# Seven block products instead of eight in the up projection of an MLP, with the residual kept in DRAM

## The chip, the core and the metric

The kernel runs on one core of a Trainium2 chip. What counts is the device time of one execution, in microseconds (us). The engines of the core work side by side, each through its own list of instructions in order: TensorE (PE; its weight loads are listed as PEld), VectorE (DVE), ScalarE (ACT), GpSimd (POOL) and SyncE (SP). TensorE reads SBUF and writes PSUM, which has eight banks of 512 float32 columns; VectorE and ScalarE read both. Transfers between DRAM and SBUF are started from the queues of SP, ACT and POOL.

## The reference

One layer of a decoder with 512 tokens and 2048 features, all in float32. A gated linear attention mixer comes first, then the MLP, then a gated embedding and a last norm. The MLP, which the change is about, is:

```python
def sq_relu_mlp(u, w_up, w_down):
    return jnp.square(jax.nn.relu(u @ w_up)) @ w_down
...
        h = h + mix.astype(h.dtype)
        h = h + sq_relu_mlp(rmsnorm(h, norm_mlp[i]), w_up[i], w_down[i])
```

`w_up` is 2048 x 8192 and `w_down` 8192 x 2048. `rmsnorm` divides each token by the root mean square of its features and multiplies by a gain.

## The kernel before

**Three products for one.** To reach float32 accuracy, each operand is split exactly into two parts of a shorter type, float32r: `hi`, a cast on ScalarE, and `lo`, the rest, a subtraction on VectorE. `mm3` (L134 to L138) then adds up hi·hi, hi·lo and lo·hi. Each of these matmuls names its stationary tile (128 x 128 of the weights in the MLP) and streams the other operand.

**Weights.** `load_w` (L122) loads a block of 512 KB, four k tiles of 128 rows x 256 columns, on SP's queue (three buffers, `raw`), casts it on ScalarE (`whi`, four buffers) and subtracts on VectorE (`wlo`, four buffers).

**Projections.** `proj_a` (L147) makes 256 output features at a time for all 512 tokens: two PSUM banks of 128 features x 512 tokens, over all k tiles, 24 matmuls for each block of weights; then `evac` reads the banks. The banks come from two pools: `mm` with six and `at` with two.

**The MLP.** After the output projection, `evac_out` (L677) adds the residual x, which lies in DRAM (`xT_d`), and keeps the sum `h` in eight SBUF tiles. `gain_split` multiplies it by the gain and splits it into `U`; the token's root mean square is put in later, as the row `r2`. The hidden features are taken in eight slices of 1024 (FFC, L31). For each slice the up projection (L705) runs over 16 k tiles; `evac_up` multiplies by `r2` with the relu, squares and splits into `S`. Then the down projection (L712) runs over the slice's eight k tiles, and `evac_dn` adds to `h` in place. The last slice also makes the gain and split for the next stage, the gate projection, whose last two column groups are 256 wide (GROUPS, L737).

**Order.** The program order is that of the loops, but the framework that builds the kernel lays out each engine's list itself: it takes an instruction when its inputs and its buffer are due, earlier instructions of the program first. It also sets all semaphores, and gives out buffers of a pool as they come free. The largest pool is `spool` with 34 slots of 4 KB per partition.

## Time and profile before

| what | before |
|---|---|
| median of 3 runs | 2435.47 us (2435.34 to 2437.28) |
| the profiled execution: its span, first to last instruction | 2433.7 us (the only time that is given for it) |
| TensorE busy | 2416.9 us, 99% |
| VectorE busy | 1049.6 us, 43% |
| ScalarE busy | 720.3 us, 30% |
| moved by DMA | 248 MB, 102 GB/s |

The profile comes from one more execution, so its span is set beside the median and not taken for it. Busy time is counted for each engine by itself; the engines overlap. An engine's idle time is put down to what ended it. Names are those of the program, with buffer numbers left out: `ps_up` stands for all PSUM tiles of the up projection. A line number is that of the innermost helper, so L136 to L138 are the three matmuls of `mm3` wherever they are called.

### The profile page before, as it was taken

To read this page: it belongs to the slowest core of one execution; us is meant where nothing else is said; L and a number is where in the kernel's file an instruction comes from. 1 tells how busy PE (TensorE), PEld (TensorE's weight loads), DVE (VectorE), ACT (ScalarE), POOL (GpSimd) and SP (SyncE) were. 2 spreads that over 40 slices of the span, in tenths; PEclk is the share of its full clock that TensorE was granted. 3 is DMA by queue.
4 is the path that set the end of the run, shared out by engine and by line. 5 is a ranking of instruction groups with operands and counts; after the bars stand their busy time and mean duration, and the time that the engine had idled before them with its cause. 6 is when DMAs were issued, how large, how long until landed. Compare 5 with 4: busy or idle time off the path is not lost.

```text
span 2433.7 us, 26605 instructions
## 1 busy us (share of the span) xinstructions
PE 2416.9 (99%) x11056; PEld 2010.0 (83%) x11056; DVE 1049.6 (43%) x1402; ACT 720.3 (30%) x923; POOL 42.9 (2%) x79
## 2 busy tenths in 40 slices
PE   9999999999999999999999999999999999999998
PEld 7888888888888888888888888888888888888888
DVE  6655647446644433333333333333333333354344
ACT  5433324333433321221222221221221222233322
POOL 3000000000100000000000000000000000000000
PEclk9999999999999999999999999999999999999999
DMA  7323323223344333333333323333333333333222
GB/s 256 100 78 109 87 78 104 87 91 91 119 128 126 119 101 97 95 95 96 98 101 96 96 95 97 102 96 95 95 96 99 100 96 95 104 97 115 91 78 79
DMA packets 219017, 248.18 MB, mean 102 GB/s; under 512 B 8308, under 2 KB 197424, under 8 KB 218896
## 3 DMA queue, kind: packets, MB, share of 16 engines
q1 hardware_dynamic: 213344, 228.68, 30.8%
q0 software_dynamic: 5520, 17.79, 2.2%
q8 instruction: 86, 1.41, 0.2%
q14 instruction: 35, 0.29, 0.0%
q10 hardware_dynamic: 32, 0.01, 0.0%
HBM read 234.91 MB, written 11.53 MB: 101 GB/s over the span
## 4 chain that ended last, share of the span: by engine, by line
PE 87%; issue 11%; DMA 0%; DVE 0%; POOL 0%; ACT 0%; SPq 0%; ACTq 0%; POOLq 0%
PE ps_up L136 10%; PE ps_up L138 10%; PE ps_dn L138 10%; PE ps_dn L137 10%; PE ps_dn L136 10%; PE ps_up L137 10%; PE ps_g L136 2%; PE ps_g L138 2%; PE ps_g L137 2%; PE ps_wo L137 2%; PE ps_wo L138 2%; PE ps_wo L136 2%; PE ps_v L136 1%; PE ps_v L137 1%; PE ps_og L137 1%
## 5 line engine op out<-in xcount | busy, mean ns | idle before, releaser
L136 PE MATMUL ps_up<-U_norm_mlp,whi_up 128*128 128x512 f32 x1024 | 398.9, 390 | 0.0
L138 PE MATMUL ps_up<-U_norm_mlp,wlo_up 128*128 128x512 f32 x1024 | 398.4, 389 | 0.0
L137 PE MATMUL ps_up<-U_norm_mlp,whi_up 128*128 128x512 f32 x1024 | 398.3, 389 | 0.0
L136 PE MATMUL ps_dn<-S,whi_dn 128*128 128x512 f32 x1024 | 398.3, 389 | 0.0
L137 PE MATMUL ps_dn<-S,whi_dn 128*128 128x512 f32 x1024 | 398.3, 389 | 0.0
L138 PE MATMUL ps_dn<-S,wlo_dn 128*128 128x512 f32 x1024 | 398.3, 389 | 0.0
L128 DVE TENSOR_TENSOR wlo_up<-raw_up,whi_up 128x1024 fp32r<-128x1024 f32 x128 | 156.8, 1225 | 347.3 <-ACT whi_up L126 347.3
L126 ACT CAST whi_up<-raw_up 128x1024 fp32r<-128x1024 f32 x128 | 135.0, 1055 | 519.6 <-PE ps_up L137 380.2
L126 ACT CAST whi_dn<-raw_dn 128x1024 fp32r<-128x1024 f32 x128 | 135.0, 1054 | 516.7 <-PE ps_dn L137 384.6
L128 DVE TENSOR_TENSOR wlo_dn<-raw_dn,whi_dn 128x1024 fp32r<-128x1024 f32 x128 | 156.8, 1225 | 275.2 <-ACT whi_dn L126 275.2
L137 PEld LDWEIGHTS ps_up<-U_norm_mlp,whi_up 128*128 128x128 f32 x1024 | 192.2, 188 | 40.1 <-issue 0.2
L138 PEld LDWEIGHTS ps_up<-U_norm_mlp,wlo_up 128*128 128x128 f32 x1024 | 192.2, 188 | 40.0
L136 PEld LDWEIGHTS ps_up<-U_norm_mlp,whi_up 128*128 128x128 f32 x1024 | 192.2, 188 | 40.0 <-issue 0.2
L137 PEld LDWEIGHTS ps_dn<-S,whi_dn 128*128 128x128 f32 x1024 | 192.2, 188 | 39.9
L138 PEld LDWEIGHTS ps_dn<-S,wlo_dn 128*128 128x128 f32 x1024 | 192.2, 188 | 39.9
L136 PEld LDWEIGHTS ps_dn<-S,whi_dn 128*128 128x128 f32 x1024 | 192.2, 188 | 39.9
L708 DVE TENSOR_TENSOR h<-h,ps_dn 128x512 f32<-128x512 f32 x128 | 87.5, 687 | 170.9 <-PE ps_dn L138 170.9
L136 PE MATMUL ps_g<-whi_wg,U_norm_ple 128*128 128x512 f32 (+1 forms) x320 | 112.0, 350 | 0.0
L138 PE MATMUL ps_g<-whi_wg,U_norm_ple 128*128 128x512 f32 (+1 forms) x320 | 111.3, 348 | 0.0
L137 PE MATMUL ps_g<-wlo_wg,U_norm_ple 128*128 128x512 f32 (+1 forms) x320 | 111.2, 348 | 0.0
L136 PE MATMUL ps_og<-X,whi_og 128*128 128x512 f32 x256 | 102.5, 400 | 0.0
L136 PE MATMUL ps_v<-whi_v,X 128*128 128x512 f32 x256 | 100.8, 394 | 0.0
(270 smaller groups left out, 3307.9 us busy)
## 6 DMA issues: line engine op xcount, KB each, us to landing
raw_up<-in_w_up SPq DMA_DIRECT2D x128, 512.0 KB, 3.7
raw_dn<-in_w_down SPq DMA_DIRECT2D x128, 512.0 KB, 3.6
raw_v<-in_gla_w_in SPq DMA_DIRECT2D x32, 512.0 KB, 3.8
raw_og<-in_gla_w_in SPq DMA_DIRECT2D x32, 512.0 KB, 3.8
raw_wo<-in_gla_w_out SPq DMA_DIRECT2D x32, 512.0 KB, 3.5
raw_wg<-in_w_ple_gate SPq DMA_DIRECT2D x32, 512.0 KB, 3.7
raw_q<-in_gla_w_in SPq DMA_DIRECT2D x12, 512.0 KB, 3.7
raw_k<-in_gla_w_in SPq DMA_DIRECT2D x12, 512.0 KB, 3.8
```

What stands on the lines that cost most here:

```text
L126: nc.scalar.copy(hi, raw)
L128: nc.vector.tensor_tensor(out=lo, in0=raw, in1=hi.bitcast(F32), op=ALU.subtract)
L136: nc.tensor.matmul(ps, lhsT=wa[0], rhs=wb[0], start=first, stop=False)
L137: nc.tensor.matmul(ps, lhsT=wa[0], rhs=wb[1], start=False, stop=False)
L138: nc.tensor.matmul(ps, lhsT=wa[1], rhs=wb[0], start=False, stop=last)
L708: nc.vector.tensor_tensor(out=h_of(i), in0=h_of(i), in1=ps, op=ALU.add)
```

## The change

The up projection is computed by Strassen's scheme on 2 x 2 blocks: two k tiles by two feature tiles of the weights, and two k tiles by two halves of 256 tokens of the input. Seven block products take the place of eight. They need sums and differences of blocks on both sides.

- **The input's side**, once: `operands` makes four differences of the scaled residual for each pair of k tiles, and splits these and three of the blocks themselves. The root mean square of the attention's input (`rb`) is put in here, and its inverse (`rinv`) later, in `r2`. This stands in the output projection's `evac_out`, for the last three pairs behind it.
- **The weights' side**, for each of 32 groups of 256 features: `up_group` loads blocks of 512 KB as before. VectorE makes four sums for each pair of k tiles (three operations for two pairs, in one buffer, `sum`). ScalarE casts three blocks and four sums for each pair, VectorE subtracts. 21 matmuls of 256 columns follow for each pair. The seven products lie in halves of four PSUM banks.
- **The evacuation**: a copy on ScalarE and five operations on VectorE put the four output blocks together, then relu with `r2`, square and split as before, on 1024 columns at once.
- **The slices** become 16 chunks of 512 hidden features. A chunk's two up groups alternate with the eight down groups of the chunk before: block, block, down, block, down, block, down, evacuation, down, and the same again. The first chunk has no down groups, the last round only these.
- **The residual** no longer lies in SBUF. `evac_out` stores it to a new DRAM tensor `h_d`; each down group loads its two tiles (256 x 512) on POOL's queue, adds its two banks, and stores them back. The last chunk keeps them in SBUF. Even down groups take banks from `mm`, odd ones from `at`.
- **Room**: some buffers of the attention are closed before the MLP, the buffers for temporaries are fewer, and the memory for POOL's descriptors is a quarter of what it was. One early load of many small pieces, `lr_raw`, moves from POOL's queue to ScalarE's.

```diff
-FFC = 1024
+FFC = 512
+NKP = NK // 2
+HT = T // 2
...
+    h_d = dram.tile([NK, P, T], F32, name="h_d")
...
             lr_raw = slot([P, NK, RANK], "lr_raw")
-            nc.gpsimd.dma_start(lr_raw, w_in[:, 6144:6160].rearrange("(k p) c -> p k c", p=P))
+            nc.scalar.dma_start(lr_raw, w_in[:, 6144:6160].rearrange("(k p) c -> p k c", p=P))
...
+            nc.vector.tensor_scalar(out=rinv, in0=ssum, scalar1=1.0 / D, scalar2=EPS, op0=ALU.mult, op1=ALU.add)
+            nc.vector.tensor_tensor(out=rinv, in0=rinv, in1=rtok, op=ALU.mult)
             bcast(rtok, rb, "x")
...
     scope.close()
-    tpool = ctx.enter_context(tc.tile_pool(name="tpool", bufs=6))
+    mlp = ExitStack()
+    tpool = mlp.enter_context(tc.tile_pool(name="tpool", bufs=1))
+    def extra(shape, name, dtype=F32):
+        return spool2.tile(shape, dtype, tag="e", name=name)
+    def wide(name):
+        return tpool.tile([P, 8, HT], F32, tag="w", name=name)
+    def sums(name):
+        return tpool.tile([P, 2, 4, P], F32, tag="sum", name=name)
...
+    def operand_slots(kp):
+        a_ = [slot([P, 4, HT], f"XS{p}_{kp}", F32R) for p in range(2)]
+        if kp % 2 == 0:
+            b_ = [slot([P, 4, HT], f"XA{p}_{kp}", F32R) for p in range(2)]
+            spare[kp + 1] = b_
+            runs = [[(0, 3, b_[p][:, 0:3, :])] for p in range(2)]
+        else:
+            e = slot([P, 4, HT], f"XA_{kp}", F32R)
...
+    def operands(kp, u):
+        a_, runs = operand_slots(kp)
+        ub = u.rearrange("p k (h t) -> p (k h) t", h=2)
+        d = sums(f"D_{kp}").rearrange("p a b c -> p (a b c)").rearrange("p (o t) -> p o t", t=HT)
+        nc.vector.tensor_tensor(out=d[:, 0, :], in0=ub[:, 1, :], in1=ub[:, 3, :], op=ALU.subtract)
+        nc.vector.tensor_tensor(out=d[:, 1, :], in0=ub[:, 0, :], in1=ub[:, 1, :], op=ALU.subtract)
+        nc.vector.tensor_tensor(out=d[:, 2, :], in0=ub[:, 0, :], in1=d[:, 0, :], op=ALU.subtract)
+        nc.vector.tensor_tensor(out=d[:, 3, :], in0=ub[:, 2, :], in1=d[:, 2, :], op=ALU.subtract)
+        for n_run in range(len(runs[0])):
+            o, n, hi = runs[0][n_run]
+            lo = runs[1][n_run][2]
+            for q_ in range(n):
+                blk = (0, 2, 3)[o + q_]
+                if q_ and (0, 2, 3)[o + q_ - 1] == blk - 1:
+                    continue
+                m = 2 if q_ + 1 < n and (0, 2, 3)[o + q_ + 1] == blk + 1 else 1
+                src = ub[:, blk:blk + m, :]
+                nc.scalar.copy(hi[:, q_:q_ + m, :], src)
+                nc.vector.tensor_tensor(
+                    out=lo[:, q_:q_ + m, :], in0=src, in1=hi[:, q_:q_ + m, :].bitcast(F32), op=ALU.subtract)
+        nc.scalar.copy(a_[0], d)
+        nc.vector.tensor_tensor(out=a_[1], in0=d, in1=a_[0].bitcast(F32), op=ALU.subtract)
+    late = {}
+    def evac_out(i, ps):
+        kp = i // 2
+        if i % 2 == 0:
+            late["x"] = load([P, 2, T], f"xres_{kp}")
+            nc.gpsimd.dma_start(late["x"], xT_d[i:i + 2].rearrange("k p t -> p k t"))
+            if kp in (5, 6):
+                late["u"] = extra([P, 2, T], f"u_{kp}")
+            else:
+                late["u"] = wide(f"u_{kp}").rearrange("p a t -> p (a t)").rearrange("p (a t) -> p a t", t=T)[:, 0:2, :]
+            late[kp] = late["u"]
+        h = late["x"][:, i % 2, :]
+        nc.vector.tensor_tensor(out=h, in0=ps, in1=h, op=ALU.add)
+        nc.vector.scalar_tensor_tensor(
+            out=late["u"][:, i % 2, :], in0=h, scalar=vec("norm_mlp", i), in1=rb, op0=ALU.mult, op1=ALU.mult)
+        add_squares(h, f"mlp_{i}", i == 0)
+        if i % 2:
+            nc.gpsimd.dma_start(h_d[i - 1:i + 1].rearrange("k p t -> p k t"), late["x"])
+            if kp < 5:
+                operands(kp, late["u"])
+    w_out = a["gla_w_out"].rearrange("o k c -> (o k) c")
+    proj_a(w_out, 0, GH, 0, D, evac_out, None, "wo")
+    for kp in (5, 6, 7):
+        operands(kp, late[kp])
+    r2 = const.tile([P, T], F32, name="r2")
+    rt2 = tiny([P, NTT], "rt2")
+    nc.vector.tensor_tensor(out=rt2, in0=rstd_of(token_sums(acc2, "mlp"), D, NTT, "mlp"), in1=rinv, op=ALU.mult)
+    bcast(rt2, r2, "mlp")
...
+    B11, B22, B21, T1, T3, T2, T4 = range(1, 8)
+    S1, S3, R2, R4, A11, A12, A22 = range(7)
+    PRODUCTS = ((A11, B11), (R2, T2), (S3, T3), (S1, T1), (A12, B21), (R4, B22), (A22, T4))
+    BANK = ((0, 0), (0, 1), (1, 0), (1, 1), (2, 0), (2, 1), (3, 0))
+    def up_group(g):
+        ps = [bank(f"ps_up{g}_{b}").rearrange("p (a t) -> p a t", a=2) for b in range(4)]
+        for k4 in range(NK // 4):
+            raw = wpool.tile([P, 4, 256], F32, tag="raw", name=f"raw_up{g}_{k4}", bufs=3)
+            nc.sync.dma_start(raw, w_rows(w_up, 4 * k4, 4, 256 * g, 256))
+            rp = raw.rearrange("p (q k) (n c) -> p q (k n) c", q=2, n=2)
+            t = sums(f"T{g}_{k4}")
+            nc.vector.tensor_tensor(
+                out=t[:, :, 0:2, :], in0=rp[:, :, 1:3, :], in1=rp[:, :, 0:1, :].broadcast_to([P, 2, 2, P]), op=ALU.add)
+            nc.vector.tensor_tensor(out=t[:, :, 2, :], in0=t[:, :, 0, :], in1=rp[:, :, 2, :], op=ALU.add)
+            nc.vector.tensor_tensor(out=t[:, :, 3, :], in0=t[:, :, 2, :], in1=rp[:, :, 3, :], op=ALU.add)
+            for q_ in range(2):
+                kp = 2 * k4 + q_
+                hi = wpool.tile([P, 8, P], F32R, tag="whi", name=f"whi_up{g}_{kp}")
+                lo = wpool.tile([P, 8, P], F32R, tag="wlo", name=f"wlo_up{g}_{kp}")
+                for o, src in ((1, rp[:, q_, 1:4, :]), (4, t[:, q_, :, :])):
+                    n = src.shape[1]
+                    nc.scalar.copy(hi[:, o:o + n, :], src)
+                    nc.vector.tensor_tensor(
+                        out=lo[:, o:o + n, :], in0=src, in1=hi[:, o:o + n, :].bitcast(F32), op=ALU.subtract)
+                for n, (xa, wb) in enumerate(PRODUCTS):
+                    b, half = BANK[n]
+                    xh, xl = OPS[kp][xa]
+                    dst = ps[b][:, half, :]
+                    nc.tensor.matmul(dst, lhsT=hi[:, wb, :], rhs=xh, start=kp == 0 and half == 0, stop=False)
+                    nc.tensor.matmul(dst, lhsT=hi[:, wb, :], rhs=xl, start=False, stop=False)
+                    nc.tensor.matmul(dst, lhsT=lo[:, wb, :], rhs=xh, start=False, stop=kp == NKP - 1 and (b == 3 or half == 1))
+            yield
+        e = wide(f"e_{g}")
+        nc.scalar.copy(e[:, 4, :], ps[0][:, 0, :])
+        nc.vector.tensor_tensor(out=e[:, 7, :], in0=ps[0][:, 1, :], in1=e[:, 4, :], op=ALU.subtract)
+        nc.vector.tensor_tensor(out=e[:, 6, :], in0=e[:, 7, :], in1=ps[1][:, 0, :], op=ALU.subtract)
+        nc.vector.tensor_tensor(
+            out=e[:, 3:6:2, :], in0=ps[1][:, 1:2, :].broadcast_to([P, 2, HT]), in1=e[:, 6:8, :], op=ALU.add)
+        nc.vector.tensor_tensor(out=e[:, 0:3:2, :], in0=ps[2], in1=e[:, 4:6, :], op=ALU.add)
+        nc.vector.tensor_tensor(out=e[:, 1, :], in0=ps[3][:, 0, :], in1=e[:, 6, :], op=ALU.subtract)
+        z = e[:, 0:4, :].rearrange("p (f h) t -> p f (h t)", f=2)
+        nc.vector.scalar_tensor_tensor(
+            out=z, in0=z, scalar=0.0, in1=r2.unsqueeze(1).broadcast_to([P, 2, T]), op0=ALU.max, op1=ALU.mult)
+        nc.scalar.activation(out=z, in_=z, func=AF.Square)
+        sh = slot([P, 2, T], f"Sh_{g}", F32R)
+        sl = slot([P, 2, T], f"Sl_{g}", F32R)
+        nc.scalar.copy(sh, z)
+        nc.vector.tensor_tensor(out=sl, in0=z, in1=sh.bitcast(F32), op=ALU.subtract)
+        S[g] = (sh, sl)
...
+        add_squares(
+            h_of(i), f"{norm}_{i}", first, lambda n: sums(n).rearrange("p a b c -> p (a b c)")[:, i % 2 * T:i % 2 * T + T])
+    def down_group(c, g):
+        last = c == NS - 1
+        ps = [(at if g % 2 else mm).tile([P, T], F32, tag="at" if g % 2 else "mm", name=f"ps_dn{c}_{g}_{i}")
+              for i in range(2)]
+        hs = (slot if last else load)([P, 2, T], f"h_{c}_{g}")
+        nc.gpsimd.dma_start(hs, h_d[2 * g:2 * g + 2].rearrange("k p t -> p k t"))
+        hi, lo = load_w(w_rows(w_dn, NFK * c, NFK, 256 * g, 256), [P, NFK, 256], f"dn{c}_{g}")
+        for kk in range(NFK):
+            sh, sl = S[2 * c + kk // 2]
+            for i in range(2):
+                s = slice(i * P, (i + 1) * P)
+                f = 1 - kk % 2
+                mm3(ps[i], (hi[:, kk, s], lo[:, kk, s]), (sh[:, f, :], sl[:, f, :]), kk == 0, kk == NFK - 1)
+        for i in range(2):
+            nc.vector.tensor_tensor(out=hs[:, i, :], in0=hs[:, i, :], in1=ps[i], op=ALU.add)
+        if last:
+            h1[g] = hs
+            for i in range(2):
+                gain_split(2 * g + i, "norm_ple", 2 * g + i == 0)
         else:
...
+            nc.gpsimd.dma_start(h_d[2 * g:2 * g + 2].rearrange("k p t -> p k t"), hs)
+    for c in range(NS + 1):
+        ups = [] if c == NS else [u for g in range(2) for u in [up_group(2 * c + g)]]
+        downs = iter(range(8 if c else 0))
+        def down():
+            g = next(downs, None)
+            if g is not None:
+                down_group(c - 1, g)
+        for half in range(2):
+            if ups:
+                u = ups[half]
+                next(u)
+                for _ in range(3):
+                    next(u)
+                    down()
+                next(u)
+            down()
+            if not ups:
+                for _ in range(3):
+                    down()
+    mlp.close()
+    gpool = ctx.enter_context(tc.tile_pool(name="gpool", bufs=6))
...
-    nc = _bacc.Bacc("TRN2", target_bir_lowering=False, num_devices=1, dynamic_dma_scratch_size=4096)
+    nc = _bacc.Bacc("TRN2", target_bir_lowering=False, num_devices=1, dynamic_dma_scratch_size=1024)
```

## Rows read from the trace of the kernel before

**Rows 1.** The page: busy us (share of span) and instructions; the clock line.
```profile
PE 2416.9 (99%) x11056; PEld 2010.0 (83%) x11056; DVE 1049.6 (43%) x1402; ACT 720.3 (30%) x923; POOL 42.9 (2%) x79
...
PEclk9999999999999999999999999999999999999999
```

**Rows 2.** Stretches: length, busy PE, PEld, DVE, ACT, POOL; clock, DMA share, GB/s.
```profile
0.00:60.00 60.00, 54.54 (x249) 43.56 (x250) 35.93 (x49) 34.35 (x90) 18.94 (x35) 0.94 0.80 256
...
819.00:2213.00 1394.00, 1393.92 (x6151) 1153.41 (x6150) 507.55 (x556) 354.61 (x417) 1.84 (x3) 1.00 0.32 99
```

**Rows 3.** Waits of TensorE, first and last of six: total us, times, longest.
```profile
PE ps_qk L137 <- DVE X L241: 1.3, 1, 1.3
...
PE ps_bc_o L212 <- DVE dg_o L208: 0.5, 1, 0.5
```

**Rows 4.** Groups by line, TensorE: busy us, mean ns, idle before.
```profile
L136 PE MATMUL ps_up<-U_norm_mlp,whi_up 128*128 128x512 f32 x1024 | 398.9, 390 | 0.0
```

**Rows 5.** Timeline of TensorE at 1500 us (start, duration), 16 rows apart inclusive.
```profile
1500.06 0.39 PE L136 MATMUL ps_dn<-S,whi_dn 128*128 128x512 f32 x1
...
1503.46 0.39 PE L136 MATMUL ps_dn<-S,whi_dn 128*128 128x512 f32 x1
```

**Rows 6.** Timeline of TensorE in the gate stage, first and last of 44.
```profile
2373.73 0.28 PE L136 MATMUL ps_g<-whi_wg,U_norm_ple 128*128 128x256 f32 x1
...
2378.89 0.28 PE L137 MATMUL ps_g<-wlo_wg,U_norm_ple 128*128 128x256 f32 x1
```

**Rows 7.** Timeline of TensorE's weight loads in the same stage, two neighbours.
```profile
2384.90 0.19 PEld L137 LDWEIGHTS ps_g<-wlo_wg,U_norm_ple 128*128 128x128 f32 x1
2385.02 0.19 PEld L138 LDWEIGHTS ps_g<-whi_wg,U_norm_ple 128*128 128x128 f32 x1
```

**Rows 8.** Groups by line and shape, VectorE: busy us, mean ns, idle before.
```profile
L128 DVE TENSOR_TENSOR wlo_up<-raw_up,whi_up 128x1024 fp32r<-128x1024 f32 x128 | 156.8, 1225 | 347.3 <-ACT whi_up L126 347.3
...
L708 DVE TENSOR_TENSOR h<-h,ps_dn 128x512 f32<-128x512 f32 x128 | 87.5, 687 | 170.9 <-PE ps_dn L138 170.9
...
L764 DVE TENSOR_TENSOR gate<-gate,ps_ple 128x256 f32<-128x256 f32 x8 | 3.4, 420 | 13.3 <-ACT gate L763 8.6 <-PE ps_ple L757 4.7
```

**Rows 9.** The same view, ScalarE.
```profile
L126 ACT CAST whi_up<-raw_up 128x1024 fp32r<-128x1024 f32 x128 | 135.0, 1055 | 519.6 <-PE ps_up L137 380.2 <-PE ps_dn L137 122.8 <-PE ps_wo L137 13.2
...
L763 ACT ACTIVATE gate<-ps_g,r 128x256 f32<-128x256 f32 x8 | 3.5, 473 | 9.3 <-PE ps_g L138 9.3
```

**Rows 10.** Timeline of VectorE behind the last down group (idle before, releaser).
```profile
2214.48 1.22 DVE L128 TENSOR_TENSOR wlo_wg<-raw_wg,whi_wg 128x1024 fp32r<-128x1024 f32 x1 [0.21 <-ACT whi_wg L126]
...
2216.28 0.68 DVE L675 TENSOR_TENSOR acc<-acc,sq_norm_ple 128x512 f32<-128x512 f32 x1
2216.89 0.74 DVE L666 SCALAR_TENSOR_TENSOR U_norm_ple<-h,vcols,U_norm_ple 128x512 fp32r<-128x512 f32 x1
```

**Rows 11.** Waits of all engines: total us, times, longest.
```profile
ACT whi_up L126 <- PE ps_up L137: 380.2, 95, 4.4
```

**Rows 12.** Timeline of POOL.
```profile
224.35 1.20 POOL L579 DMA_DIRECT2D gr<-gated_d  x2 [0.48 <-DMA gated_d<-y]
...
372.00 2.35 POOL L615 DMA_DIRECT2D gated_d<-y  x4 [146.45 <-DVE y L613]
```

**Rows 13.** The page, DMA issues: count, KB each, median us to landing.
```profile
raw_up<-in_w_up SPq DMA_DIRECT2D x128, 512.0 KB, 3.7
...
raw_qk<-in_gla_w_in SPq DMA_DIRECT2D x8, 512.0 KB, 6.3
xT_d<-xr POOLq DMA_DIRECT2D x16, 256.0 KB, 4.6
...
nf<-in_norm_final POOLq DMA_DIRECT2D x2, 512.0 KB, 5.3
```

**Rows 14.** Timeline of VectorE after the output projection.
```profile
824.39 0.16 DVE L183 TENSOR_SCALAR ms_mlp<-ps_ts_mlp 128x4 f32<-128x4 f32 x1 [1.21 <-PE ps_ts_mlp L202]
```

**Rows 15.** Timeline of POOL in the first 60 us.
```profile
9.69 1.18 POOL L311 DMA_DIRECT2D lr_raw<-in_gla_w_in  x1
```

More of the change, by code (lines that the diff above doesn't have):

```diff
@@ L107, in vec @@
         return vcols[:, VOFF[n] + k:VOFF[n] + k + 1]
[L109 to L111 removed]
+    restart = acon.tile([P, T], F32, name="restart")
+    masks = acon.tile([P, 384 * len(QUARTERS) + T], U8, name="masks")
+    att_diag = acon.tile([P, T], F32, name="att_diag")
     warm = bank("ps_warm")
@@ L219, in trunk_kernel @@
     rtok = const.tile([P, NTT], F32, name="rtok")
+    rinv = const.tile([P, NTT], F32, name="rinv")
     ssq = const.tile([P, 8, NTT], F32, name="ssq")
@@ new lines, in sums, with add_squares @@
+    def sums(name):
+        return tpool.tile([P, 2, 4, P], F32, tag="sum", name=name)
+    acc2 = const.tile([P, T], F32, name="acc2")
+    def add_squares(src, name, first, temp=temp):
+        if first:
+            nc.scalar.activation(out=acc2, in_=src, func=AF.Square)
+        else:
+            sq = temp(f"sq_{name}")
+            nc.scalar.activation(out=sq, in_=src, func=AF.Square)
+            nc.vector.tensor_tensor(out=acc2, in0=acc2, in1=sq, op=ALU.add)
+    OPS = [None] * NKP
+    spare = {}
@@ new lines, in operand_slots @@
+    def operand_slots(kp):
[6 more added lines that the diff above has]
+            e = slot([P, 4, HT], f"XA_{kp}", F32R)
+            b_ = spare[kp]
+            runs = [[(0, 2, e[:, 2 * p:2 * p + 2, :]), (2, 1, b_[p][:, 3:4, :])] for p in range(2)]
+        where = [[a_[p][:, o, :] for o in range(4)] for p in range(2)]
+        for p in range(2):
+            for o, n, ap in runs[p]:
+                where[p] += [ap[:, q_, :] for q_ in range(n)]
+        OPS[kp] = [(where[0][o], where[1][o]) for o in range(7)]
+        return a_, runs
@@ L656, in h_of @@
+    S = {}
+    NS = DFF // FFC
+    h1 = [None] * (NK // 2)
     def h_of(i):
         return h1[i // 2][:, i % 2, :]
-    U = [None] * NK
-    acc2 = const.tile([P, T], F32, name="acc2")
     def gain_split(i, norm, first):
@@ L669, in gain_split @@
         U[i] = t
-        if first:
-            nc.scalar.activation(out=acc2, in_=h_of(i), func=AF.Square)
-        else:
-            sq = temp(f"sq_{norm}_{i}")
-            nc.scalar.activation(out=sq, in_=h_of(i), func=AF.Square)
-            nc.vector.tensor_tensor(out=acc2, in0=acc2, in1=sq, op=ALU.add)
-    def evac_out(i, ps):
-        xr = load([P, T], f"xres_{i}")
-        nc.gpsimd.dma_start(xr, xT_d[i])
-        nc.vector.tensor_tensor(out=h_of(i), in0=ps, in1=xr, op=ALU.add)
-        gain_split(i, "norm_mlp", i == 0)
@@ L683, in trunk_kernel @@
-    w_out = a["gla_w_out"].rearrange("o k c -> (o k) c")
-    proj_a(w_out, 0, GH, 0, D, evac_out, None, "wo")
-    r2 = const.tile([P, T], F32, name="r2")
-    bcast(rstd_of(token_sums(acc2, "mlp"), D, NTT, "mlp"), r2, "mlp")
-    w_up = a["w_up"].rearrange("o k c -> (o k) c")
-    w_dn = a["w_down"].rearrange("o k c -> (o k) c")
-    UM = U
-    U = [None] * NK
-    for c in range(DFF // FFC):
-        S = [None] * NFK
-        def evac_up(i, ps):
-            z = temp(f"z_{c}_{i}")
-            nc.vector.scalar_tensor_tensor(out=z, in0=ps, scalar=0.0, in1=r2, op0=ALU.max, op1=ALU.mult)
-            nc.scalar.activation(out=z, in_=z, func=AF.Square)
-            t = slot([P, 2, T], f"S_{c}_{i}", F32R)
-            nc.scalar.copy(t[:, 0, :], z)
-            nc.vector.tensor_tensor(out=t[:, 1, :], in0=z, in1=t[:, 0, :].bitcast(F32), op=ALU.subtract)
-            S[i] = t
-        proj_a(w_up, 0, UM, FFC * c, FFC, evac_up, None, f"up{c}_")
-        def evac_dn(i, ps):
-            nc.vector.tensor_tensor(out=h_of(i), in0=h_of(i), in1=ps, op=ALU.add)
-            if c == DFF // FFC - 1:
-                gain_split(i, "norm_ple", i == 0)
-        proj_a(w_dn, NFK * c, S, 0, D, evac_dn, None, f"dn{c}_")
@@ L714, in trunk_kernel, with temp @@
+    mlp.close()
+    gpool = ctx.enter_context(tc.tile_pool(name="gpool", bufs=6))
+    def temp(name):
+        return gpool.tile([P, T], F32, tag="t", name=name)
     r3 = const.tile([P, NTT], F32, name="r3")
```

11 lines of the change are left out of this document (7 added, 4 removed).

## The prediction

> **What bounds the kernel now.** [...] Then the stretches: from 819 to 2213 us, where the up and down projections run, TensorE is busy 1393.9 of 1394 us, VectorE 507.6 and ScalarE 354.6 [rows 2]. Then the waits of TensorE itself: six in the whole run, 6.0 us together, all outside that stretch [rows 3]. So in the MLP the time is a number of matmuls times a pace, and what another engine does costs nothing until it makes TensorE wait. The mean duration of a matmul is no pace (390 ns [rows 4]), since they overlap; I take the distance between starts. For 512 columns it is (1503.46 - 1500.06) / 15 = 0.2267 us [rows 5].
>
> The span is 2433.7 us; the three runs have a median of 2435.5, so some 1.8 us lie around the span. I sum against the span and add these 1.8 at the end.
>
> **The change part by part.**
>
> *Matmuls of the up projection.* Removed: three lines of 1024 each, of which one is shown [rows 4], 3072 x 0.2267 = 696.3 us. Added: 32 groups x 8 pairs of k tiles x 7 products x 3 = 5376 of 256 columns. The kernel before has such matmuls in its gate stage, with another stationary tile for each: start to start (2378.89 - 2373.73) / 43 = 0.1200 us, without a jump [rows 6]. 5376 x 0.1200 = 645.1 us, a gain of 51.2 us. Seven eighths of 696.3 would be 609.3: the other 36 us are lost because half the columns take 0.53 of the time. The down projection keeps 16 x 8 x 24 = 3072 matmuls of 512 columns.
>
> A weight load takes 0.19 us, longer than this pace, but the loads start 0.12 us apart, so they overlap one another and the matmuls [rows 7]. [...]
>
> *VectorE.* Durations: 1024 elements 1.225 us, 512 0.687, 256 0.42, the last two with an input in PSUM [rows 8] (512 from SBUF alone 0.68 [rows 10]); 384 lies halfway, 0.555. A block of weights (4 k tiles x 256 columns) needed one subtraction of 1.225. Now: three sums (0.687 + 2 x 0.42) and four subtractions (2 x 0.555 + 2 x 0.687), 4.0 us, beside 42 x 0.12 = 5.04 us of TensorE. The evacuation of a group: three operations of 256, two of 512, two of 1024 = 1.26 + 1.37 + 2.45 = 5.1 us. A down group: one subtraction and two additions, 1.225 + 1.37 = 2.6 us beside 24 x 0.2267 = 5.44. A chunk has 8 blocks, 2 evacuations and 8 down groups: 32.1 + 10.2 + 20.8 = 63.1 us, beside 40.3 + 43.5 = 83.8 us of TensorE. That is 75%, from 36% before, and an upper figure: back to back, an operation that lasts 0.68 us is followed by the next after 0.61 [rows 10]. Four waits of 0.2 us on ScalarE in a block, as in the first of these rows, would add 6.4 us, still below 83.8. ScalarE, linear between 256 elements at 0.47 and 1024 at 1.055 [rows 9]: 2 x (0.57 + 0.67) a block, 0.47 + 2 x 1.055 an evacuation, 1.055 a down group = 33 us. Both are hidden in the loop; if VectorE went beyond 83.8, each us more would cost 16.
>
> *What TensorE waits for in the loop.* Four weight buffers were four blocks of 5.44 us; now an up block takes two of them, for 2.5 us each, so they hold 10 to 13 us of work ahead instead of 21.8. Before, ScalarE mostly had to wait for TensorE to free one (95 of 128 times in this row alone, up to 4.4 us [rows 11]), so the preparation ran as early as buffers allowed. In the densest place (two down groups, then two up blocks, 21.0 us of TensorE) VectorE owes an evacuation, two pairs of additions, three blocks and the weights of a down group, 5.1 + 2.7 + 12.0 + 1.2 = 21.0 us by durations, and the third of these blocks is due only 5 us later. I take 0; more is a rival. PSUM: a group holds four of six banks, and the two down groups between it and the next, 10.9 us, cover a read-out of about 3.1 us (0.47 + 3 x 0.42 + 2 x 0.69).
>
> *The residual through DRAM.* 128 loads and 120 stores of 512 KB in the loop, all on POOL's queue, 130 MB, and another 8 stores in the output projection: traffic doubles from 99 GB/s [rows 2]. The first 60 us carried 256 GB/s, where a 512 KB load landed after 6.3 us instead of 3.7 [rows 2, 13]; three raw buffers of about 5 us each cover that. On POOL's queue a 256 KB store landed after 4.6 and a 512 KB load after 5.3 us [rows 13]. A store waits for the additions, and the next load stands behind it if the order is the program's. It need not be: the loads of gated_d were issued at 224 us, after the stores of their own rows alone, while stores to other rows of that tensor came at 372 [rows 12]. So dependences go by rows and loads are laid out ahead. With three buffers a load is out about 10 us or more before its addition, against 5.3. Cost 0; if it came late, VectorE would stand at the addition with the next weights behind it, and the 10 to 13 us of prepared weights are the cover.
>
> *The edges.* In the output projection each pair of tiles adds 4.0 us of operands to VectorE (four of 256, then 256 + 512 + 1024), 13 us in 21.8 of TensorE: hidden, except for the last pair. From its end to the first down group TensorE has ten up blocks, 50.4 us. VectorE owes the last pair's additions, scalings and squares (six operations of 512, 4.1), its operands 4.0, the statistics (some thirteen operations of 0.16 us, 0.2 with what lies between them, and one of 512: 3.2 [rows 14]), nine blocks 36.1 and two evacuations 10.2 = 57.6. By durations TensorE waits 7 us; with the 0.07 us that each of some 90 operations is shorter back to back, 1. I take 5. In that stretch two group ends have no down group to cover the banks: with two banks free, the third and fourth are needed after 12 and 18 matmuls (1.4 and 2.2 us) and read out after 0.47 + 0.42 = 0.9 and 0.9 + 0.42 + 0.69 = 2.0 us, plus two or three hand-overs of about 0.2: 1 us for both ends. At the other end eight down groups run alone, VectorE at 1.225 + 1.37 + 4 x 0.687 = 5.3 of 5.44 us, after a last evacuation: 0 to 5, I take 2. At the start the low-rank weights are issued by ScalarE instead of POOL, where the issue took 1.18 us [rows 15]: 0 to 1.2 on an engine for which TensorE waits there [rows 3], or a little below 0 if they land earlier; I take 0.5. POOL's smaller ring delays only POOL, which is 2% busy: 0.
>
> **Sum:** 2433.7 - 51.2 + 5 + 1 + 2 + 0.5 = 2391.0 us of span, 2392.8 with what lies around it. Forecast 2393 us.
>
> **The rivals.**
>
> *The banks are read out late (slower).* The evacuation is VectorE's work among weights and additions. If it is laid out behind the additions of the second down group, the read-out starts 1.37 us after that group, when the next up group wants its banks. The banks then come free 1.37 + 0.9 = 2.3 and 1.37 + 2.0 = 3.4 us after that group's end. With two others free TensorE waits 0.8 and 0.4 us for these two, 1.2 an end; with none, 2.3 and 0.4, 2.7. Over 32 ends that is 38 to 86 us: 2431 to 2479, at the middle 2455. It decides from 42 / 32 = 1.3 us an end. For it: VectorE is twice as busy as before and takes its work in order. Against: the group is complete 10.9 us earlier, and additions not yet due needn't stand ahead of a read-out that is.
>
> *Weights come late.* With 10 to 13 us prepared, a long run of VectorE's work or a late addition makes TensorE wait 0.5 to 1.2 us per half chunk: 16 to 38 us, 2409 to 2431, at the middle 2418. For it: one buffer for the sums, chained through ScalarE. Against: 25% of VectorE is free.
>
> *The products don't keep the pace.* From 696.3 / 5376 = 0.1295 us each nothing is gained; at 0.128 the time is 2393 + 43 = 2436. For it: two products share a bank, and four parts of a weight tile come from different instructions. Against: the exact 0.1200.
>
> *Loads on the path.* If no load overlapped the next, each matmul would take at least 0.19 us [rows 7]: 5376 x 0.07 = 376 us more, 2769. [...]
>
> **How the numbers follow.** Forecast 0.68 (2384 to 2410: no cost at the edges, or three times the 8.5 us); late weights 0.12; late banks 0.11; pace 0.04; loads 0.02; the rest, 0.03, I give to something slower that I don't see. Faster by over 0.2%, about what a measurement of this kernel can tell from no change: 0.68 + 0.12 = 0.80. Within 0.2%: 0.05, the pace and the lower end of the late banks. Slower: 0.15. For 8 in 10 the range takes the forecast and the late weights: from 2382, just below 2435.5 - 51.2 = 2384, to 2430.
>
> **What the profile after would show.** Right: matmuls of ps_up 0.12 us apart, TensorE busy about 2366 us and never waiting inside the loop; VectorE about 1600 us (1050 - 242 for the old up work + 88 additions + 514 blocks + 163 evacuations + 32 operands); waits of TensorE for VectorE or ScalarE only around the start of the up projection and of the gate stage. Late banks: TensorE waits for VectorE's read-out at 32 places. Late weights: for whi or wlo. Another pace shows in the starts. What would make it wrong: any wait that comes back in each chunk, since 2.7 us a chunk takes the whole gain.

## The result, and the profile after

The kernel with seven products takes 2397.55 us (median of 4 runs, 2395.81 to 2398.59); the kernel before, beside it, 2435.40 us. The ratio is 0.9843, with a 95% interval from 0.9829 to 0.9857: 37.9 us faster, 4.6 us more than the 2393 us of the forecast and inside its range.

The page of the kernel after: span, busy us of each engine (share of the span) and instructions, the clock row, and the chain that ended last.

```profile
span 2395.1 us, 33417 instructions
...
PE 2368.7 (99%) x13360; PEld 2079.5 (87%) x13360; DVE 1552.7 (65%) x2457; ACT 869.2 (36%) x1287; POOL 222.5 (9%) x326
...
PEclk9999999999999999999999999999999999999999
...
PE 98%; DVE 1%; DMA 0%; issue 0%; ACT 0%; SPq 0%; ACTq 0%
```

As in [rows 1], TensorE is busy for 99% of the span, and the chain that ended last is 98% TensorE. VectorE went from 1049.6 to 1552.7 us and makes up 1% of that chain.

The stretches of the kernel after (length, busy PE, PEld, DVE, ACT, POOL; clock, DMA share, GB/s), to be read beside [rows 2]:

```profile
818.00:870.00 52.00, 43.42 (x331) 41.69 (x330) 46.38 (x96) 24.01 (x44) 1.44 (x2) 0.90 0.33 103
870.00:2150.00 1280.00, 1280.00 (x8022) 1162.52 (x8021) 920.27 (x1430) 460.57 (x706) 175.71 (x245) 1.00 0.63 203
```

From 870 to 2150 us TensorE is busy all the time at a granted clock of 1.00, with VectorE at 920.27 / 1280 = 72% and twice the traffic of before. What is new and bad stands in the first row: 8.6 us without work for TensorE and a mean granted clock of 0.90, just where the up projection begins. The waits of TensorE (total us, times, longest) name it; the first two of eight, against the six of [rows 3]:

```profile
PE ps_up L797 <- ACT whi_up L790: 5.2, 1, 5.2
PE ps_ts_mlp L206 <- DVE acc L679: 3.4, 1, 3.4
```

The other six, of 1.7 us and less, lie at the start of the kernel, before the MLP.

**Where the 38.6 us of span went.** I measure between starts of matmuls. From the first of `ps_up` to the last of `ps_dn` it was 818.32 to 2213.15 = 1394.8 us before and is 818.58 to 2174.99 = 1356.4 after: 38.4 less. Ahead of that stretch 0.3 us were added, behind it 220.1 us are left instead of 220.6. So gain and loss are as good as all in the MLP, and they divide into three:

- the count of matmuls at their paces: -51.2 us, as worked out in the prediction;
- +0.06 us in each half chunk with down groups (one up group and the four down groups that alternate with it, see below), 30 of them: +1.8;
- what is left, -38.4 + 51.2 - 1.8 = 11.0 us, lies at the start of the up projection.

**The loop.** ScalarE's timeline in the kernel after (start, duration): the copy that opens the evacuation of each up group.

```profile
1321.67 0.37 ACT L803 COPY e<-ps_up 128x256 f32<-128x256 f32 x1
...
1363.65 0.37 ACT L803 COPY e<-ps_up 128x256 f32<-128x256 f32 x1
```

One half chunk takes 41.98 us, and so it does in every one from the third group on. It has 168 matmuls of 256 columns and 96 of 512: 168 x 0.1200 + 96 x 0.2267 = 20.16 + 21.76 = 41.92 us. The other 0.06 us come where the width changes. TensorE's timeline in the kernel after, around one down group:

```profile
1386.13 0.40 PE L140 MATMUL ps_dn<-Sh,whi_dn 128*128 128x512 f32 x1
1386.36 0.40 PE L141 MATMUL ps_dn<-Sl,whi_dn 128*128 128x512 f32 x1
1386.60 0.39 PE L142 MATMUL ps_dn<-Sh,wlo_dn 128*128 128x512 f32 x1
...
1391.60 0.28 PE L797 MATMUL ps_up<-XA,whi_up 128*128 128x256 f32 x1
1391.71 0.28 PE L798 MATMUL ps_up<-XA,whi_up 128*128 128x256 f32 x1
```

The first matmuls of 512 columns start 0.23 and 0.24 us apart, and the 24 of them take 1391.60 - 1386.13 = 5.47 us instead of 5.44; the step that follows is 0.11 instead of 0.12. With four down groups in a half, that makes 0.06.

**The start.** VectorE's timeline in the kernel after, then ScalarE's and TensorE's (start, duration, in brackets the idle time before it and what ended it):

```profile
806.61 1.23 DVE L726 TENSOR_TENSOR XS<-D,XS 128x1024 fp32r<-128x1024 f32 x1 [0.68 <-PE ps_wo L142]
808.22 0.56 DVE L791 TENSOR_TENSOR wlo_up<-raw_up,whi_up 128x384 fp32r<-128x384 f32 x1 [0.39 <-ACT whi_up L790]
813.66 0.56 DVE L791 TENSOR_TENSOR wlo_up<-raw_up,whi_up 128x384 fp32r<-128x384 f32 x1 [4.88 <-ACT whi_up L790]
818.10 1.37 DVE L742 TENSOR_TENSOR xres<-ps_wo,xres 128x512 f32<-128x512 f32 x2 [3.88 <-PE ps_wo L142]
...
825.12 1.23 DVE L726 TENSOR_TENSOR XS<-D,XS 128x1024 fp32r<-128x1024 f32 x1
...
826.38 0.69 DVE L780 TENSOR_TENSOR T<-raw_up 128x512 f32<-128x512 f32 x1
```

```profile
828.02 1.14 ACT L790 CAST whi_up<-T 128x512 fp32r<-128x512 f32 x2 [2.93 <-DVE T L783]
```

```profile
822.48 1.02 PE L206 MATMUL ps_ts_mlp<-ones,acc 128*128 128x1 f32 x8 [3.39 <-DVE acc L679]
828.69 0.58 PE L797 MATMUL ps_up<-XS,whi_up 128*128 128x256 f32 x1 [5.19 <-ACT whi_up L790]
829.07 0.41 PE L798 MATMUL ps_up<-XS,whi_up 128*128 128x256 f32 x1
829.28 0.41 PE L797 MATMUL ps_up<-XS,whi_up 128*128 128x256 f32 x1
...
834.02 0.28 PE L799 MATMUL ps_up<-XS,wlo_up 128*128 128x256 f32 x1
834.14 0.28 PE L797 MATMUL ps_up<-XA,whi_up 128*128 128x256 f32 x1
```

VectorE prepares the first weight blocks' `raw_up` part before 818 us (the rows at 808.22 and 813.66), but not one sum `T`. The first `T` starts at 826.38, as the last reader of `D_7` ends (825.12 + 1.23 = 826.35). `D` and `T` are tiles of the same one buffer, `sum`, and `D_7` stands ahead of the first `T` in the program; `D_7` itself can't be made until the last pair of the output projection is there, at 818. So from 807.8 (806.61 + 1.23, the last reader of `D_6`) the buffer was kept for a tile that was not due yet, while VectorE sat idle for 4.88 and 3.88 us with nothing else to do. Of the first seven products TensorE had run the first, whose weights are no sum. The second needs a sum, and two others that need none stand behind it in the list. So, but for the statistics' short matmuls at 822.48, TensorE stood still until 828.69.

### The profile page after: what moved, and what is told of

Same layout as the page of the kernel before. It is cut to its first block, busy times and chain, and to the rows that moved or that the text cites. A ratio compares the mean times of both kernels' runs of the same rounds, so it can differ in the third digit from the quotient of the medians.

```text
span 2395.1 us, 33417 instructions
## 1 busy us (share of the span) xinstructions
PE 2368.7 (99%) x13360; PEld 2079.5 (87%) x13360; DVE 1552.7 (65%) x2457; ACT 869.2 (36%) x1287; POOL 222.5 (9%) x326
## 4 chain that ended last, share of the span: by engine, by line
PE 98%; DVE 1%; DMA 0%; issue 0%; ACT 0%; SPq 0%; ACTq 0%
PE ps_dn L140 10%; PE ps_dn L141 10%; PE ps_dn L142 10%; PE ps_up L799 9%; PE ps_up L797 9%; PE ps_up L798 9%; PE ps_g L142 2%; PE ps_v L140 2%; PE ps_g L140 2%; PE ps_g L141 2%; PE ps_wo L140 2%; PE ps_wo L141 2%; PE ps_og L140 2%; PE ps_og L142 2%; PE ps_og L141 2%; PE ps_v L142 2%
## 5 line engine op out<-in xcount | busy, mean ns | idle before, releaser
L140 PE MATMUL ps_dn<-Sh,whi_dn 128*128 128x512 f32 x1024 | 399.5, 390 | 0.0
L141 PE MATMUL ps_dn<-Sl,whi_dn 128*128 128x512 f32 x1024 | 399.4, 390 | 0.0
L142 PE MATMUL ps_dn<-Sh,wlo_dn 128*128 128x512 f32 x1024 | 398.3, 389 | 0.0
L797 PE MATMUL ps_up<-XS,whi_up 128*128 128x256 f32 x1024 | 290.5, 284 | 5.2 <-ACT whi_up L790 5.2
L799 PE MATMUL ps_up<-XS,wlo_up 128*128 128x256 f32 x1024 | 290.4, 284 | 0.0
L798 PE MATMUL ps_up<-XS,whi_up 128*128 128x256 f32 x1024 | 290.3, 283 | 0.0
L140 PEld LDWEIGHTS ps_dn<-Sh,whi_dn 128*128 128x128 f32 x1024 | 192.6, 188 | 37.6
L799 PE MATMUL ps_up<-XA,wlo_up 128*128 128x256 f32 x768 | 218.3, 284 | 0.0
L798 PE MATMUL ps_up<-XA,whi_up 128*128 128x256 f32 x768 | 217.4, 283 | 0.0
L797 PE MATMUL ps_up<-XA,whi_up 128*128 128x256 f32 x768 | 217.0, 283 | 0.0
L797 PEld LDWEIGHTS ps_up<-XS,whi_up 128*128 128x128 f32 x1024 | 197.1, 192 | 5.8 <-ACT whi_up L790 5.3
L798 PEld LDWEIGHTS ps_up<-XS,whi_up 128*128 128x128 f32 x1024 | 197.2, 193 | 0.0
L799 PEld LDWEIGHTS ps_up<-XS,wlo_up 128*128 128x128 f32 x1024 | 197.1, 192 | 0.1
```

The costliest lines, as they stand in the source:

```text
L140: nc.tensor.matmul(ps, lhsT=wa[0], rhs=wb[0], start=first, stop=False)
L141: nc.tensor.matmul(ps, lhsT=wa[0], rhs=wb[1], start=False, stop=False)
L142: nc.tensor.matmul(ps, lhsT=wa[1], rhs=wb[0], start=False, stop=last)
L797: nc.tensor.matmul(dst, lhsT=hi[:, wb, :], rhs=xh, start=kp == 0 and half == 0, stop=False)
L798: nc.tensor.matmul(dst, lhsT=hi[:, wb, :], rhs=xl, start=False, stop=False)
L799: nc.tensor.matmul(dst, lhsT=lo[:, wb, :], rhs=xh, start=False, stop=kp == NKP - 1 and (b == 3 or half == 1))
```

## The experiments

My theory after these readings: the loop costs what its matmuls cost, at 256 columns a little over half of 512; everything else in it is hidden; and the loss at the start is one of order, made by the shared buffer. The rivals were that the loss at the start is VectorE's amount of work, as the prediction had costed it; that the streamed residual or the alternation costs or saves something; and that VectorE is close to making TensorE wait in the loop. `e1_sum_apart`, `e2_eight_512` and `e3_eight_256` are medians of 4, 10 and 4 executions, with intervals; the others are one execution each, set beside the 2397.55 us of after. The four executions of after spread over 2.8 us, so smaller differences of a single one say nothing.

### The last pair's differences in a buffer of their own

```diff
-        d = sums(f"D_{kp}").rearrange("p a b c -> p (a b c)").rearrange("p (o t) -> p o t", t=HT)
+        if kp == 7:
+            d = extra([P, 4, HT], f"D_{kp}")
+        else:
+            d = sums(f"D_{kp}").rearrange("p a b c -> p (a b c)").rearrange("p (o t) -> p o t", t=HT)
```

> The four differences of the last pair of k tiles get a buffer of their own; until now they and the sums of the weights shared the one buffer of the tag sum. Theory (order): in the changed kernel the first block's sums stood behind these differences, so TensorE waited 3.4 + 5.2 us at the start of the up projection and lost some 2.7 us more at the lower clock; VectorE was idle 4.9 and 3.9 us just before. With the buffer apart these sums are made in that idle time: the two waits shrink to 0 to 3 us together, the granted clock of the stretch 818 to 870 us rises from 0.90 to 0.95 or more, and the time falls by 8 to 11 us from 2397.6, to 2387 to 2390. Rival (amount, my own step in the prediction): VectorE simply has some 57 us of work beside 50 us of TensorE there; no work goes away, so the waits stay within 2 us of what they are and the time at 2395 to 2398.

Measured: 2387.15 us (2385.24 to 2387.99), ratio to before 0.9802, interval 0.9788 to 0.9817, which does not touch that of the kernel after. VectorE's timeline and the stretch at the start in this kernel:

```profile
808.15 0.69 DVE L783 TENSOR_TENSOR T<-raw_up 128x512 f32<-128x512 f32 x1
...
812.12 0.69 DVE L783 TENSOR_TENSOR T<-raw_up 128x512 f32<-128x512 f32 x1
```

```profile
818.00:870.00 52.00, 51.96 (x414) 50.46 (x413) 47.98 (x99) 26.26 (x47) 1.44 (x2) 1.00 0.34 107
```

The sums of the first two blocks move into the time in which VectorE had been idle, both waits of TensorE are gone (the longest left is 1.6 us, at the start of the kernel), and the clock stays at 1.00. VectorE does the same work as before, so the loss came from the order that the shared buffer forced on it. The MLP goes from 1356.4 to 2164.78 - 818.86 = 1345.9 us, which leaves 1345.9 - 1394.8 + 51.2 - 1.8 = 0.5 us of loss at the start where after has 11.0. This kernel is faster than both.

### Eight products in the new order: 512 columns and 256

Both keep the chunks of 512, the alternation, the stream through DRAM and the buffers, and take the eight plain products with no sums. A group then needs two PSUM banks instead of four, and its read-out is shorter. `e2_eight_512` has the old 96 matmuls of 512 columns in a group, 24 for each block of weights; `e3_eight_256` takes each in two halves of 256 columns, so its up projection has 6144 matmuls.

```diff
+            hi, lo = load_w(w_rows(w_up, 4 * k4, 4, 256 * g, 256), [P, 4, 256], f"up{g}_{k4}")
+            for kk in range(4):
+                kp = 2 * k4 + kk // 2
+                xh, xl = OPS[kp][0][:, kk % 2, :], OPS[kp][1][:, kk % 2, :]
+                for i in range(2):
+                    s = slice(i * P, (i + 1) * P)
...
+                    mm3(ps[i], (hi[:, kk, s], lo[:, kk, s]), (xh, xl), k4 == 0 and kk == 0, k4 == 3 and kk == 3)
...
+                    for h in range(2):
+                        ts_ = slice(h * HT, (h + 1) * HT)
+                        mm3(ps[i][:, ts_], (hi[:, kk, s], lo[:, kk, s]), (xh[:, ts_], xl[:, ts_]),
+                            k4 == 0 and kk == 0 and h == 0, k4 == 3 and kk == 3 and h == 1)
```

The first `mm3` is that of `e2_eight_512`, the loop over `h` that of `e3_eight_256`.

> The up projection with all eight products, 512 columns each (3072 matmuls), no sums and differences; chunks of 512, alternation with the down groups and the residual through DRAM stay. Theory: only the number of matmuls and their pace count, and stream and alternation are hidden. Then TensorE is busy 2417 us as in the kernel before and the time is 2434 to 2441 (2397.6 less the 11 us lost at the start, plus 51.2). Rival: the new arrangement itself has a price or a gain, and the seven products bring more or less than 51.2 us; each us of it shows as a distance from 2435.

> As e2_eight_512, but every product in two halves of 256 columns: 6144 matmuls. Theory: 0.1200 us each, 737.3 instead of 696.3 us, so 41 us more than e2_eight_512: 2475 to 2482. It shows the price of the halved width alone; seven instead of eight products would then be worth 92 us and the width takes 41 back. Rival: the pace of 0.1200 holds in the gate stage alone, and the distance is something else.

Measured: 2436.17 us, ratio 1.0004 (0.9994 to 1.0013), and 2479.79 us, ratio 1.0181 (1.0164 to 1.0198). VectorE's timeline, two evacuations in a row, in `e2_eight_512` and then in `e3_eight_256`:

```profile
1330.27 1.37 DVE L771 SCALAR_TENSOR_TENSOR e<-ps_up,r 128x512 f32<-128x512 f32 x2 [2.68 <-PE ps_up L142]
...
1373.79 1.37 DVE L771 SCALAR_TENSOR_TENSOR e<-ps_up,r 128x512 f32<-128x512 f32 x2 [2.68 <-PE ps_up L142]
```

```profile
1352.19 1.41 DVE L774 SCALAR_TENSOR_TENSOR e<-ps_up,r 128x512 f32<-128x512 f32 x2 [2.95 <-PE ps_up L142]
...
1397.05 1.41 DVE L774 SCALAR_TENSOR_TENSOR e<-ps_up,r 128x512 f32<-128x512 f32 x2 [2.95 <-PE ps_up L142]
```

The first is the pace of 512 columns, 43.52 / 192 = 0.22667 us, with no remainder where the width does not change. The second, 44.86 us, is 192 x 0.12 + 21.76 = 44.80 and again 0.06 for the changes of width. So the change has three separate prices. What it carries along (smaller chunks, alternation, 130 MB through DRAM, the smaller memory for descriptors and the early load on ScalarE's queue) costs nothing: `e2_eight_512` is level with the kernel before within 0.13%. Half the columns cost 2479.79 - 2436.17 = 43.6 us. One product fewer in eight, at that width, is worth 2479.79 - 2387.15 = 92.6 us where the start is in order (`e1_sum_apart`), and 82.2 as the change was made. These are differences of medians; from the first matmul of `ps_up` to the last of `ps_dn`, in the profiled executions, they are 42.8 and 91.6 us, beside 41.0 + 1.8 and 92.2 by the count.

### The stream with fewer buffers

The first kernel takes the residual's tiles from a pool of two buffers and was to hold one of them for another tile; the second has one fixed tile for all loads of the loop.

```diff
+    hold = extra([P, 2, T], "hold")
+    nc.gpsimd.memset(hold[:, 0, 0:1], 0.0)
...
-        hs = (slot if last else load)([P, 2, T], f"h_{c}_{g}")
+        hs = (slot if last else extra)([P, 2, T], f"h_{c}_{g}")
+        if c == NS - 2 and g == 7:
+            nc.gpsimd.memset(hold[:, 0, 0:1], 0.0)
```

> The residual's tiles in the loop take one buffer in turn instead of three, so each load waits for the store before it to land. Theory: the residual's stream was hidden by loads some 20 us ahead. With one buffer a chain of additions 1.4, store 4.0, load 4.3 and hand-overs of about 0.6, 10.3 us a down group, stands beside 10.5 us of TensorE: it is just hidden or costs up to 10 us in all (2397 to 2408). Rival (late loads): the additions stand in VectorE's list with the next weights behind them, so TensorE waits in each chunk, 2 us or more: 2430 and above.

Measured: 2398.04 us, every half chunk of the loop as before. But POOL's timeline in this kernel shows that it did not do what it was made for:

```profile
803.74 0.10 POOL L848 MEMSET hold<- 128x1 f32 x1
804.25 0.72 POOL L849 DMA_DIRECT2D h<-h_d  x1 [0.41 <-POOL hold L848]
```

The second use of `hold`, written just ahead of the last load of the loop, waits for nothing and was laid out at 803.74, before the first load. Its buffer was free from then on, and the loads use both. So the run says only that two buffers do as well as three, and I made the fixed tile:

```diff
+    h_one = extra([P, 2, T], "h_one")
...
-        hs = (slot if last else load)([P, 2, T], f"h_{c}_{g}")
+        hs = slot([P, 2, T], f"h_{c}_{g}") if last else h_one
```

> One fixed tile takes every load of the residual in the loop, so a load cannot be issued before the store of the group before has read it. (In e4_h_one two buffers were in use in the end, since the second was given free at once.) Theory: a chain of additions 1.4, store about 4.0, load 4.3 and hand-overs 0.6 takes 10.3 us for each down group beside 10.5 us of TensorE on average; two neighbouring down groups stand only 5.4 us apart, and VectorE also has other work between, so the chain gets longer than the work and TensorE waits at last: 0.5 to 3 us a down group, 2400 to 2460. Rival (hidden anyway by the spare banks and the weights made ahead): no wait in the loop, a half chunk stays at 41.98 us, 2396 to 2399.

Measured: 2428.65 us, 31.1 more than after (32.5 more from the first matmul of `ps_up` to the last of `ps_dn`). Groups by line and shape in this kernel, then its waits (total us, times, longest):

```profile
L855 DVE TENSOR_TENSOR h_one<-h_one,ps_dn 128x512 f32<-128x512 f32 x240 | 154.9, 684 | 219.7 <-DMA h_one<-h_d 196.1 <-PE ps_dn L142 13.9 <-PE ps_up L800 5.6
```

```profile
DVE T L781 <- DMA raw_up<-in_w_up: 124.3, 58, 3.6
...
PE ps_dn L142 <- DVE wlo_dn L132: 18.3, 17, 2.6
```

VectorE stands at the addition for a load that could not be issued until the store before it had landed, and the weights behind it come late to TensorE. Raw weights, whose buffers VectorE frees, come late as well: VectorE waits 124.3 us for them, 13.2 in the kernel after. The half chunks stay at 41.98 up to 1194 us; the next three take 42.5, 43.8 and 46.5. So the stream is hidden because loads run ahead, not because it is small. In the kernel after, POOL's timeline shows the distance:

```profile
1407.37 0.71 POOL L845 DMA_DIRECT2D h<-h_d  x1 [3.25 <-DMA h_d<-h]
```

With three buffers in turn, the load at 1407.37, which waited for a store out of its buffer to land, is the one whose addition comes at 1433.1, some 26 us later, and loads land after 4.3 us.

### VectorE's subtractions twice and three times

Work is repeated here. `e5_lo_half_twice` repeats the subtraction on the sums alone, the other two all of the up projection's.

```diff
-                    nc.vector.tensor_tensor(
-                        out=lo[:, o:o + n, :], in0=src, in1=hi[:, o:o + n, :].bitcast(F32), op=ALU.subtract)
+                    for _ in range(2 if o == 4 else 1):
+                        nc.vector.tensor_tensor(
+                            out=lo[:, o:o + n, :], in0=src, in1=hi[:, o:o + n, :].bitcast(F32), op=ALU.subtract)
```

`range(2)` and `range(3)` stand there in `e6_lo_twice` and `e7_lo_thrice`.

> VectorE's subtraction for the four sums is done twice, 2 x 0.69 us more in each block of weights; nothing else changes. Theory (amount): VectorE goes from 60.4 to 71.4 us a chunk beside 83.96 of TensorE, so the loop keeps 41.98 us a half chunk, and only the ten blocks at the start, where VectorE was full, lose 5 to 10 us: 2402 to 2410. Rival (late weights): the chain from sums to cast to subtraction with 10 to 13 us made ahead is already tight, and a half chunk gets longer by 1 us or more: 2430 and above.

> All four subtractions of a block are done twice, 2.48 us more: VectorE 80.3 us a chunk by durations, some 78 back to back, beside 83.96. Theory (amount): still 41.98 us a half chunk, and 15 to 20 us lost at the start: 2412 to 2420. Rival (late weights): at 93 to 96% of VectorE the order of its work decides, a half chunk takes 43 us or more: 2445 and above.

> All four subtractions three times: VectorE 100 us a chunk by durations, 95 back to back, beside 83.96 of TensorE. Both theories say that VectorE is now the bound; by the amount a half chunk takes 47.5 to 50 us instead of 41.98, with 25 to 35 us lost at the start: 2580 to 2665. More than that would be waits on top of the amount.

Measured: 2406.09, 2405.43 and 2521.99 us. The stretch from 870 to 2140 us in `e6_lo_twice`, and in `e7_lo_thrice`:

```profile
870.00:2140.00 1270.00, 1267.31 (x7977) 1151.73 (x7977) 1136.30 (x1908) 451.68 (x698) 170.01 (x237) 1.00 0.60 199
```

```profile
870.00:2140.00 1270.00, 1209.59 (x7383) 1069.85 (x7384) 1265.14 (x2224) 423.36 (x646) 155.64 (x217) 1.00 0.55 182
```

With VectorE at 1136.30 / 1270 = 89%, TensorE loses 2.7 us in this stretch, all before 890 us, and the half chunks are 41.98 from 952 us on, as they are in `e5_lo_half_twice`. So late weights in the loop were not near; the added time lies at the start. There the amount of work counts after all, as the stretch from 800 to 955 us shows in `e5_lo_half_twice`, then in `e6_lo_twice`:

```profile
800.00:955.00 155.00, 143.15 (x921) 130.21 (x921) 130.62 (x236) 58.63 (x100) 11.12 (x16) 0.96 0.42 136
```

```profile
800.00:955.00 155.00, 139.24 (x907) 126.30 (x907) 139.72 (x265) 57.55 (x96) 10.04 (x14) 0.97 0.41 131
```

TensorE is idle for 11.9 and 15.8 us, against 8.6 in the kernel after. That the two times are level comes from ahead of the MLP: the first matmul of `ps_up` comes at 820.67 us in `e5_lo_half_twice` and at 817.05 in `e6_lo_twice` (818.58 in the kernel after). This shift stems from the first 60 us; from then until that matmul TensorE is busy throughout in both, to within 0.1 us. From the first matmul of `ps_up` to the last matmul of `ps_dn` they take 1363.4 and 1366.5 us, 7.0 and 10.1 more than the 1356.4 of after (1356.1 in `e4_h_one`). So `e5_lo_half_twice` is as the theory had it, and `e6_lo_twice` loses less than the 15 to 20 us expected; why was not settled. The shared buffer made the loss in the kernel after, as `e1_sum_apart` shows; with that order, more work for VectorE makes it larger.

At three times VectorE is the bound: 1265.14 of 1270 us. Its half chunk, by ScalarE's copy in `e7_lo_thrice`, and two of its neighbours on VectorE:

```profile
1384.65 0.37 ACT L804 COPY e<-ps_up 128x256 f32<-128x256 f32 x1 [0.53 <-PE ps_up L800]
...
1429.86 0.37 ACT L804 COPY e<-ps_up 128x256 f32<-128x256 f32 x1 [0.67 <-PE ps_up L800]
```

```profile
1349.82 0.68 DVE L792 TENSOR_TENSOR wlo_up<-T,whi_up 128x512 fp32r<-128x512 f32 x1
1350.42 0.55 DVE L792 TENSOR_TENSOR wlo_up<-raw_up,whi_up 128x384 fp32r<-128x384 f32 x1
1350.89 0.68 DVE L792 TENSOR_TENSOR wlo_up<-T,whi_up 128x512 fp32r<-128x512 f32 x1
```

The half chunk is 45.21 us, less than the 47.5 to 50 that I had expected, and the time lies below the 2580 to 2665. By durations a chunk would need 63.1 + 16 x 2 x (0.555 + 0.687) = 102.8 us of VectorE; it took 90.4. Back to back, operations that last 0.68 and 0.55 us start 0.60 and 0.47 apart. So the added 64 operations cost 32 x (0.60 + 0.47) = 34.2 us, and the rest, the chunk of the kernel after, is 90.4 - 34.2 = 56 us where the prediction had 63.1: 67% of TensorE's 83.96, an estimate from these rows.

## Why the prediction was right, and where it was wrong

**The pace of the matmuls: right.** 0.1200 us at 256 columns and 0.2267 at 512, as read from the kernel before in [rows 5, 6], held in the new code, and 51.2 us is what the count gives. The rival of a slower pace is refuted by the starts at 834.02 and 834.14, and by `e1_sum_apart`, whose whole MLP lies within 2.3 us of that count. So is the rival of loads on the path: a mean load of `ps_up` lasts 0.19 us in the kernel after, and 0.12 us separate the matmuls. What the sum left out is the change of width, +1.8 us.

**Nothing waits in the loop: right.** TensorE is busy throughout from 834 us to the end of the MLP, and late weights are refuted with it. VectorE was costed at 1600 us and is busy 1552.7. (The middle of that rival's 2409 to 2431 is 2420 and not 2418; nothing hangs on it.)

**Late banks: refuted.** In the loop, where two down groups lie between a group and the next, TensorE waits nowhere. For the other ends the prediction took the read-out to begin at a group's end. Between the first two groups, where no down group lies to cover it, the timelines of ScalarE, VectorE and TensorE in the kernel after show:

```profile
851.19 0.37 ACT L803 COPY e<-ps_up 128x256 f32<-128x256 f32 x1
```

```profile
851.92 0.42 DVE L804 TENSOR_TENSOR e<-ps_up,e 128x256 f32<-128x256 f32 x1
...
852.90 0.69 DVE L806 TENSOR_TENSOR e<-ps_up,e 128x512 f32<-128x512 f32 x1
```

```profile
852.01 0.28 PE L799 MATMUL ps_up<-XA,wlo_up 128*128 128x256 f32 x1
852.13 0.28 PE L797 MATMUL ps_up<-XA,whi_up 128*128 128x256 f32 x1
```

The second group begins at 852.13 (of the seven products, the last and the first of a pair are the two neighbours that both read `XA`). The copy starts 0.94 us before that, since the first bank is complete after two of the last seven products. The first two banks of the first group come free as their last readers end, at 851.92 + 0.42 = 852.34 and 852.90 + 0.69 = 853.59, and the second group wants its third and fourth 12 and 18 matmuls after its start, at 853.57 and 854.29. Its matmuls start 0.12 us apart throughout: the 1 us that I had put down for the two uncovered ends is 0.

**The residual through DRAM: right.** Loads land after 4.3 us, below the 5.3 of a load on POOL's queue in [rows 13], and stores after 3.5; `e2_eight_512` shows that the stream costs nothing, and `e4_h_one_held` that its cover is the loads ahead, 31.1 us without them.

**The edges: the step that was mis-sized, with the wrong reason.** The start of the up projection was given 5 us, from 1 to 7, because VectorE was counted to owe 57.6 us of work against 50.4 of TensorE. It cost 11.0: 3.39 and 5.19 us of idle time, and 2.4 more, which is what is left, around a stretch in which matmuls start 0.21 us apart (829.07 to 829.28) instead of 0.12, at a granted clock of 0.50. A fall of the clock was no term of the sum. The amount had been counted as if VectorE could take it in any order, from 818 us on. In the trace, two blocks' sums could have been made ahead of 818, and could not because of the shared buffer. I had named this buffer, "one buffer for the sums", but as a reason for late weights in the loop, where it costs nothing. The amount is not without weight: added to this order it cost 7.0 and 10.1 us more in `e5_lo_half_twice` and `e6_lo_twice`. The last chunk was given 2 us: VectorE's 5.3 us there fit into 5.44, TensorE has no wait in it, and the stretch behind the MLP is 0.4 us shorter than before. The start of the kernel was given 0.5 us and shows 0.3, which can't be told from nothing: in the profiled executions of the nine changed kernels the first matmul of `ps_up` comes anywhere from 817.03 to 821.71 us.

**The sum, as measured:** 2433.7 - 51.2 + 11.0 + 1.8 + 0.3 - 0.4 = 2395.2 us, beside a span of 2395.1. It closes because the 11.0 is the remainder; the check on it is `e1_sum_apart`, where 0.5 is left and the time is 10.4 us shorter. The forecast of 2391.0 lacks 6.0 us at the start and 1.8 of changing widths, and has 3.6 too much elsewhere (1 at the banks, 2 in the last chunk, 0.2 at the start of the kernel, 0.4 behind the MLP).
